# A hybrid encoder block in split fp32: seven units of its matrix products take a fifth pair of k tiles through Strassen's seven products, with four split buffers in place of five

## The chip, the cores and the metric

The kernel runs on one core of one Trainium2 chip. The time is in microseconds (us) of device time of one execution. A core has a matrix engine (PE), a vector engine (DVE), a scalar engine (ACT), a general engine (POOL) and a queue engine for transfers (SP); each takes its instructions in program order, and instructions wait for one another across engines.

## The reference

x has 256 tokens of 2048 channels. All is fp32.

```python
z = rms_norm(x) @ w_in                 # hq hf hi hg | aq ak av | gates
y_a = hgrn2(q, k, v, log_g)            # 8 heads, chunks of 64
y_b = chunk_band_attention(aq, ak, av) # 16 heads of 64
gate_a, gate_b = split(sigmoid(gates))
h = x + (gate_a * (y_a @ w_branch_a) + gate_b * (y_b @ w_branch_b)) @ w_out
u = rms_norm(h)
h = h + square(relu(u @ w_up)) @ w_down    # 2048 -> 8192 -> 2048
return rms_norm(h)
```

## The kernel before

**Split fp32.** PE multiplies in a rounded type (fp32r). An fp32 number is kept as two of these, a high part (the number, rounded by a cast) and a low part (what the cast left), and `mm3` (L138) makes one product of three matmuls, high by high, high by low (of the weights), low by high: L139, L140, L141. One such matmul is a 128x128 left tile by 128x512 weights into a PSUM bank. Activations are split once; weights are streamed from HBM and split as they come: a raw piece of 128x1024 (two k tiles of 512 columns, 512 KB) is loaded by SP (`piece`, L208), and `split` (L90) casts it to `wh` on ACT (L91) and subtracts to `wl` on DVE (L92). `parts` (L220) does this for a piece; `buf` (L201) gives the buffers, four each of `wh` and `wl`, and from unit gb0 on a fifth, in the pool "fifth", for every fifth split. A split whose buffer is still read by PE waits on ACT, and the DVE behind it.

**A unit** (class `Unit`, L774) is a product of 256 rows by 2048 k by two groups of 512 columns (n = 0 and 1), into four banks (m, n). The first eight of its 16 k tiles go by the Strassen-Winograd scheme: the eight blocks' products become seven, named by the banks they go to and the weights they take: 11A, 22A, 12C, 11D, 21A, 21B, 21D. A is the piece pair of k tiles 0 to 3 and n = 0, B of n = 1, D of k tiles 4 to 7 and n = 0, C of n = 1; each is summed in place between products, on DVE (`sums`, L843: A - B, then A - C; the signs are in the left sides) or by accumulating DMAs that POOL issues (`sent`, L848). A product is two splits of two k tiles, 12 matmuls (`product`, L807). The left sides of 22A, 12C, 21A and 21B are the sums S5, S4, S2, S7, made by `combos` (L735) and split like the rest. The other eight k tiles, 8 to 15, are plain: an item (n, (k, k+1)) is one split and 12 matmuls (`plain`, L853; `ITEMS`, L772).

**The order** is written by hand in `run` (L887): 11A, a late item of the unit before, sums A - B, 22A, the last late item and the end of the unit before (`rest`), then the "seconds" 12C and 11D (in turned order where no late item is left and the unit is not `spread`), sums A - C, a plain item, 21A, a plain item, 21B, two plain items, 21D, two plain items. The two items (1, (12, 13)) and (1, (14, 15)) go late, into the next unit. The letters of the next unit are loaded after 21A, 21B and 21D. Steps (`u.step`) put other work between: the turning and splitting of h (`h_blocks`, L1131: matmuls `tp_h` on PE, `hw` and `act_h` on DVE), or of the activations u. A scheduler keeps the order per engine nearly as written; splits and sums are issued early (`high_priority`), so that they stand ahead in their queues, and wait there for buffers.

**The units** are av, qk, ga0, ga2, gb0, gb2 (input projection, its gates), wo0, wo2 (output projection), and for each quarter qd of the 8192 hidden channels up{qd}0, up{qd}2, dn{qd}0, dn{qd}2. Where a unit's down projection ends, ACT copies the bank to `y` (L1211), and POOL adds it to h by a DMA. In gb0 and gb2 the gates of the unit before are evicted on ACT (`gate_gb`, L729). In names of tiles, `wl_up10p11D` is the low part of a piece of D in unit up10, product 11; `wl_up10r_8` that of the plain item with k tiles 8 and 9.

Of the kernel before, what the change touches and what calls it, by code (L numbers as in the profile page):

```python
# [50 lines left out]
def tile_hybrid_block(  # L51
# [714 lines left out]

    def evict(dst, acc):
        with tc.high_priority(offset=2000):
            nc.vector.tensor_tensor(dst, acc, dst, op=ALU.add)
# [3 lines left out]

    class Unit:  # L774


        def __init__(self, lhs, S, w, n0, what, done, kt0=0, apart=NC, steps=lambda: (), start=5, fresh=None, held=False, tail=False):
# [4 lines left out]
            self.raw, self.dma, self.c, self.items, self.steps = {}, {}, {}, list(ITEMS), []  # L782
# [104 lines left out]
    def run(u, then=None):  # L887
# [18 lines left out]
        if not late and not u.spread:  # L906
            seconds.reverse()
# [23 lines left out]
        u.plain(1, (8, 9))  # L931
# [10 lines left out]
        u.plain(1, (10, 11))  # L942
# [15 lines left out]
        u.plain(0, (10, 11))  # L958
# [103 lines left out]
    for gates, c, col, what, fresh in ((ga, 0, C_GA, "ga", None), (ga, 2, C_GA, "ga", None), (gb, 0, C_GB, "gb", ("21",)), (gb, 2, C_GB, "gb", ())):  # L1062
# [114 lines left out]
    for qd in range(NQ):  # L1177
# [3 lines left out]
        def turns(c0, uT=uT, rs=rs, Su=Su, blocks=blocks, qd=qd):  # L1181

            def one(c, m):
# [11 lines left out]

        for c in range(0, 4, 2):
            def done(m, n, acc, c=c, rs=rs, qd=qd):
                t = token(f"r{qd}{c}{n}{m}")
                with tc.high_priority(offset=2000):
# [117 lines left out]
```

## Time and profile before

| | |
|---|---|
| median of 3 runs | 1369.27 us (1367.44 to 1372.15) |
| the profiled execution | 1368.19 us, its span 1366.5 us |
| granted clock of PE | 0.999 |
| PE busy | 1356.7 us, 99% of the span |
| DVE busy | 1122.1 us, 82% |
| ACT busy | 948.6 us, 69% |
| POOL busy | 150.5 us, 11% |
| moved by DMA | 333.75 MB, 244 GB/s |

The profile is one execution: each row of a timeline gives the start from the span's beginning, the duration, engine, line, operation, out<-in, and in brackets the idle time before it with what ended it. Matmuls overlap, so what one costs is read from start to start. The groups' rows give busy time and the mean of one in ns. 1.7 us of the execution lie around the span.

### The profile page before, as it was taken

Reading aid. Unit: us, or ns where it says so; the run is one execution under the profiler, and the core shown is the slowest. Engines: PE = TensorE matmul, PEld = TensorE weight load, DVE = VectorE, ACT = ScalarE, POOL = GpSimd, SP = SyncE. Lnnn points to the kernel's source line nnn. Section 1 sums busy time; section 2 is a strip of 40 time slices with the busy share of each in tenths; the row PEclk is TensorE's granted clock in tenths of the full one; section 3 lists DMA queues with packets and bytes.
Section 4 is the critical chain, followed back from the end, with each engine's and each line's share of the span. In section 5 each row is a group of like instructions: output and inputs, shape, how many; then the busy total and the mean of one; then the engine's idle time right before and its main releaser. Section 6 shows DMA issues by size and latency. Waiting matters only on the chain.

```text
span 1366.5 us, 19044 instructions
## 1 busy us (share of the span) xinstructions
PE 1356.7 (99%) x6791; PEld 1123.1 (82%) x6791; DVE 1122.1 (82%) x1302; ACT 948.6 (69%) x1247; POOL 150.5 (11%) x231
## 2 busy tenths in 40 slices
PE   9999999999999999999999999999999999999997
PEld 7888888878778888888888888888888888888886
DVE  7888977887787775798998987789787888878886
ACT  6877765776777664455778766687666876668864
POOL 4000000111111000010121112100111002110210
PEclk9999999999999999999999999999999999999999
DMA  9754557788886986669899889988899888998892
GB/s 324 246 186 157 178 179 265 217 219 246 261 222 169 295 293 208 184 155 317 290 263 284 222 260 298 297 242 228 263 279 301 253 246 240 282 299 258 259 280 105
DMA packets 128895, 333.75 MB, mean 244 GB/s; under 512 B 11152, under 2 KB 12176, under 8 KB 128416
## 3 DMA queue, kind: packets, MB, share of 16 engines
q1 hardware_dynamic: 107936, 265.59, 56.4%
q0 software_dynamic: 20144, 66.14, 24.7%
q8 instruction: 53, 0.87, 0.3%
q10 hardware_dynamic: 720, 0.81, 0.2%
q14 instruction: 42, 0.34, 0.1%
HBM read 271.67 MB, written 10.49 MB: 206 GB/s over the span
## 4 chain that ended last, share of the span: by engine, by line
PE 98%; DMA 1%; ACT 0%; DVE 0%; issue 0%; SPq 0%; POOLq 0%; POOL 0%; ACTq 0%; DVEq 0%
PE acc_hf L181 2%; PE acc_hq L181 2%; PE tp_u L109 1%; PE acc_hg L139 1%; PE acc_qkc L139 1%; PE acc_hg L141 1%; PE acc_ba L141 1%; PE acc_hi L140 1%; PE acc_hi L139 1%; PE acc_bb L139 1%; PE acc_hi L141 1%; PE acc_hg L140 1%; PE acc_bb L141 1%; PE acc_ba L140 1%; PE acc_bb L140 1%; PE acc_ba L139 1%
## 5 line engine op out<-in xcount | busy, mean ns | idle before, releaser
L181 PE MATMUL acc_hf<-act_x,wh_hf 128*128 128x512 f32 x128 | 40.6, 399 | 0.4 <-DVE f L195 0.4
L181 PE MATMUL acc_hq<-act_x,wh_hq 128*128 128x512 f32 x128 | 40.5, 398 | 0.0
L91 ACT CAST wh_bb<-raw_bb 128x1024 fp32r<-128x1024 f32 x16 | 16.9, 1054 | 23.3 <-PE acc_ba L141 17.5
L92 DVE TENSOR_TENSOR wl_bb<-raw_bb,wh_bb 128x1024 fp32r<-128x1024 f32 x16 | 19.6, 1224 | 14.8 <-ACT wh_bb L91 14.7
L91 ACT CAST wh_ba<-raw_ba 128x1024 fp32r<-128x1024 f32 x16 | 16.8, 1053 | 19.9 <-PE acc_bb L141 13.8
L92 DVE TENSOR_TENSOR wl_ba<-raw_ba,wh_ba 128x1024 fp32r<-128x1024 f32 x16 | 19.6, 1223 | 10.8 <-ACT wh_ba L91 10.8
L186 PEld LDWEIGHTS acc_hq<-act_x,wl_hq 128*128 128x128 f32 x128 | 23.4, 188 | 6.1 <-DVE wl_hq L92 0.9
L186 PEld LDWEIGHTS acc_hf<-act_x,wl_hf 128*128 128x128 f32 x128 | 23.4, 188 | 6.0 <-DVE wl_hf L92 0.9
L1212 POOL DMA_DIRECT2D hd<-y x24 | 26.2, 1156 | 1.8 <-ACT y L1211 1.3
L92 DVE TENSOR_TENSOR wl_hf<-raw_hf,wh_hf 128x1024 fp32r<-128x1024 f32 (+2 forms) x21 | 20.3, 968 | 6.7 <-ACT wh_hf L91 6.7
L92 DVE TENSOR_TENSOR act_u<-tp_u,act_u 128x512 fp32r<-128x512 f32 x32 | 21.9, 685 | 4.7 <-ACT act_u L91 4.2
L139 PE MATMUL acc_bb<-wh_bb,act_yb 128*128 128x512 f32 x64 | 25.2, 393 | 0.0
L186 PE MATMUL acc_hq<-act_x,wl_hq 128*128 128x256 f32 x128 | 24.7, 280 | 0.4 <-DVE wl_hq L92 0.4
L186 PE MATMUL acc_hf<-act_x,wl_hf 128*128 128x256 f32 x128 | 24.7, 279 | 0.4 <-DVE wl_hf L92 0.4
L139 PE MATMUL acc_hg<-wh_hg,act_x 128*128 128x512 f32 x64 | 25.1, 392 | 0.0
L139 PE MATMUL acc_hi<-wh_hi,act_x 128*128 128x512 f32 x64 | 25.0, 391 | 0.0
L141 PE MATMUL acc_hg<-wh_hg,act_x 128*128 128x512 f32 x64 | 24.9, 390 | 0.0
L141 PE MATMUL acc_ba<-wh_ba,act_ya 128*128 128x512 f32 x64 | 24.9, 389 | 0.0
L141 PE MATMUL acc_hi<-wh_hi,act_x 128*128 128x512 f32 x64 | 24.9, 389 | 0.0
L140 PE MATMUL acc_hi<-wl_hi,act_x 128*128 128x512 f32 x64 | 24.9, 389 | 0.0
L140 PE MATMUL acc_hg<-wl_hg,act_x 128*128 128x512 f32 x64 | 24.9, 389 | 0.0
L139 PE MATMUL acc_ba<-wh_ba,act_ya 128*128 128x512 f32 x64 | 24.9, 389 | 0.0
(1996 smaller groups left out, 5226.6 us busy)
## 6 DMA issues: line engine op xcount, KB each, us to landing
raw_hi<-in_w_in_n_dram SPq DMA_DIRECT2D x16, 512.0 KB, 4.2
raw_hg<-in_w_in_n_dram SPq DMA_DIRECT2D x16, 512.0 KB, 4.3
raw_ba<-in_w_branch_a_dram SPq DMA_DIRECT2D x16, 512.0 KB, 4.6
raw_bb<-in_w_branch_b_dram SPq DMA_DIRECT2D x16, 512.0 KB, 4.7
raw_hf<-in_w_in_t_dram SPq DMA_DIRECT2D x12, 512.0 KB, 4.5
raw_hq<-in_w_in_t_dram SPq DMA_DIRECT2D x12, 512.0 KB, 5.5
hd<-y POOLq DMA_DIRECT2D x24, 256.0 KB, 7.4
raw_aq<-in_w_in_t_dram SPq DMA_DIRECT2D x8, 512.0 KB, 3.8
```

The costliest lines, as they stand in the source:

```text
L91: casts[:] = [(copy or nc.scalar.copy)(hi, src)]
L92: return nc.vector.tensor_tensor(lo, src, hi.bitcast(F32), op=ALU.subtract)
L109: nc.tensor.transpose(tp[:, j, :], src[:, j * P:(j + 1) * P], ident)
L139: nc.tensor.matmul(acc, hi, wh, start=first, stop=False, skip_group_check=True)
L140: nc.tensor.matmul(acc, hi, wl, start=False, stop=False, skip_group_check=True)
L141: newest[:] = [nc.tensor.matmul(acc, lo, wh, start=False, stop=last, skip_group_check=True)]
L181: newest[:] = [nc.tensor.matmul(acc[cb], wh[:, cb * P:(cb + 1) * P], r.rearrange("p u t -> p (u t)"), start=kt == 0, stop=last)]
L186: newest[:] = [nc.tensor.matmul(acc[cb][:, 0:T], wl[:, cb * P:(cb + 1) * P], r[:, 0, :], start=False, stop=False)]
L1212: nc.gpsimd.dma_start(hd[n][m], t, accum_op=ALU.add)
```

## The change

In seven units, gb2, up10, up20, up30, dn02, dn12 and dn22 (`five=True`), k tiles 8 and 9 join the Strassen part as a fifth pair, one k tile on each side. Each of the seven products then takes a fifth k tile: 7 mm3 in place of the 8 of the items (0, (8, 9)) and (1, (8, 9)). The raw pieces are the same two, of k tiles 8 and 9 for n = 0 (X) and n = 1 (Y), now loaded by `load5` into one buffer each of the pool "fifth"; a new `half` splits one k tile of them (128x512) into a buffer of full size, half of which stays empty. The sums of the fifth tiles are four adds of 128x512 a unit on DVE, issued after a product's first split (L854). `fifths` makes the fifth tiles of S5, S7, S2 and S4, once each for x, h and the u of three quarters. S7 is now kept in a part of the split left side that no product reads, and the split of that block is left out where it is made from the turns; the fourth step of x's sums comes after the product ak.

The fifth split buffer goes, for all units from gb0 on. A five unit leaves one late item in place of two, and the seconds are turned (11D ahead of 12C) where fewer than two are left; so up10, up20, up30 and up12, up22, up32 have no plain item between 22A, 11D and 12C. In five units A - C waits for the last low of the first second. PE has 5976 instructions in place of 5997 in program order, DVE 1366 for 1278, ACT 1205 for 1169; POOL and SP have as many as before. Lines move: L846 is now L890, L804 L841, L834 L878, L1211 L1266, L1142 L1194, L769 L796.

```diff
     def buf(tag, what):
-        if "fifth" in homes:
-            taken[tag] += 1
-        last = taken[tag] > 0 and taken[tag] % 5 == 0
-        return (homes["fifth"] if last else wpool).tile([P, 2 * NC], F32R, name=f"{tag}_{what}", tag=tag, bufs=1 if last else 4)
+        return wpool.tile([P, 2 * NC], F32R, name=f"{tag}_{what}", tag=tag, bufs=4)
...
+    def half(raw, a, what):
+        made = [buf(t, what)[:, 0:NC] for t in ("wh", "wl")]
+        with tc.high_priority(offset=2000):
+            lows.append(split(*[t.rearrange("p (c n) -> p c n", n=T) for t in made], view5(raw, a)))
+        return made
...
         def final(i, s):
-            t = home.tile([P, 4, 2, P], F32R, name=f"S{i}_{what}", tag=f"S{i}", bufs=1)
+            if i == 7:
+                t = lhs[0][:, :, :, P:2 * P]
+            else:
+                t = home.tile([P, 4, 2, P], F32R, name=f"S{i}_{what}", tag=f"S{i}", bufs=1)
...
+    def fifths(lhs, what, home, made):
+        a = token(f"a9_{what}").rearrange("p (j t) -> p j t", t=T)
+        x = lhs[2][:, 0:2].bitcast(F32)
+        nc.vector.tensor_tensor(a, x[:, :, 0, :], x[:, :, 1, :], op=ALU.add)
+        c = fours(token(f"c9_{what}"))
+        (a00, a10), (a01, a11) = [[a[:, j, m * P:(m + 1) * P] for m in range(NM)] for j in range(2)]
+        nc.vector.tensor_tensor(c[:, 0], a10, a11, op=ALU.subtract)
...
+        t = home.tile([P, 4, 2, P], F32R, name=f"S9_{what}", tag="S9", bufs=1)
+        split(t[:, :, 0, :], t[:, :, 1, :], c)
...
+    ITEMS5 = [(1, (10, 11)), (1, (12, 13)), (0, (10, 11)), (0, (12, 13)), (0, (14, 15)), (1, (14, 15))]
+    FIFTH = {"A": ("X", 0), "D": ("X", 1), "B": ("Y", 0), "C": ("Y", 1)}
+    SUMS5 = {("22", "A"): "B", ("21", "A"): "C", ("21", "B"): "C", ("21", "D"): "A"}
...
         def product(self, i, name, left, first=False):
...
                     wh, wl = parts(raw, f"{self.what}p{i}{name}{g}")
+                if not g and self.five and (i, name) in SUMS5:
+                    dst, src = [view5(self.raw[r], a) for r, a in (FIFTH[name], FIFTH[SUMS5[i, name]])]
+                    with tc.issue_after(lows[-1].ins), tc.high_priority(offset=2000):
+                        nc.vector.tensor_tensor(dst, dst, src, op=ALU.add)
                 for a in range(2):
                     mm3(self.c[i], *left(g + a), wh[:, a], wl[:, a], first and not g + a, False)
+            if self.five:
+                raw, a = FIFTH[name]
+                mm3(self.c[i], *left(4), *half(self.raw[raw], a, f"{self.what}p{i}{name}5"), False, False)
...
-        if not late and not u.spread:
+        if len(late) < 2 and not u.spread:
             seconds.reverse()
...
         seconds[0]()
+        behind_first = lows[-1]
         u.step(next(at))
         seconds[1]()
         with ExitStack() as es:
-            if u.spread:
-                es.enter_context(tc.issue_after(lows[-1].ins))
+            if u.spread or u.five:
+                es.enter_context(tc.issue_after((lows[-1] if u.spread else behind_first).ins))
             u.sums("A", "C")
         u.sent("D", "A")
         u.step(next(at))
-        u.plain(1, (8, 9))
+        u.plain(1, (10, 11) if u.five else (8, 9))
...
-            u.plain(0, (10, 11))
+        if not u.five:
+            u.plain(0, (10, 11))
...
         if then:
             then.load("D")
+            then.load5("X")
...
-        late.append(lambda: u.plain(1, LATE[0]))
+        if not u.five:
+            late.append(lambda: u.plain(1, LATE[0]))
         late.append(rest)
```

Three places of DVE's order are shown, before and after. First, unit up10 around its seconds: `raw_up10A` rows are the sums A - C, `_r_8` and `_r_10` the first plain item.

```order
878 L846 TENSOR_TENSOR raw_up10A_7833<-raw_up10A_7833,raw_up10C_7882 128x1024
879 L92 TENSOR_TENSOR wl_up10p12C_8080<-raw_up10C_7880,wh_up10p12C_8079 128x1024
880 L92 TENSOR_TENSOR wl_up10p12C_8090<-raw_up10C_7882,wh_up10p12C_8089 128x1024
881 L92 TENSOR_TENSOR wl_up10p11D_8100<-rawd_up10D_7939,wh_up10p11D_8099 128x1024
882 L92 TENSOR_TENSOR wl_up10p11D_8110<-rawd_up10D_7941,wh_up10p11D_8109 128x1024
883 L92 TENSOR_TENSOR wl_up10r_8_8124<-rawp_up10r_8_7975,wh_up10r_8_8123 128x1024
```

The same place after the change, with X and Y the fifth pieces:

```order
914 L92 TENSOR_TENSOR wl_up10p11D_8163<-rawd_up10D_8021,wh_up10p11D_8162 128x1024
915 L92 TENSOR_TENSOR wl_up10p11D_8173<-rawd_up10D_8023,wh_up10p11D_8172 128x1024
916 L92 TENSOR_TENSOR wl_up10p11D_8183<-rawx_up10X,wh_up10p11D_8182 128x512
917 L890 TENSOR_TENSOR raw_up10A_7915<-raw_up10A_7915,raw_up10C_7970 128x1024
918 L92 TENSOR_TENSOR wl_up10p12C_8190<-raw_up10C_7970,wh_up10p12C_8189 128x1024
919 L92 TENSOR_TENSOR wl_up10p12C_8200<-raw_up10C_7972,wh_up10p12C_8199 128x1024
920 L92 TENSOR_TENSOR wl_up10p12C_8210<-rawy_up10Y,wh_up10p12C_8209 128x512
921 L890 TENSOR_TENSOR raw_up10A_7917<-raw_up10A_7917,raw_up10C_7972 128x1024
922 L92 TENSOR_TENSOR wl_up10r_10_8221<-rawp_up10r_10_8059,wh_up10r_10_8220 128x1024
```

11D has come ahead of 12C, both sums A - C have moved between them and the plain item, and two halves have been added.

Second, unit gb2 at the same place, before and then after:

```order
558 L92 TENSOR_TENSOR wl_gb2p11D_4864<-rawd_gb2D_4707,wh_gb2p11D_4863 128x1024
559 L92 TENSOR_TENSOR wl_gb2p11D_4874<-rawd_gb2D_4709,wh_gb2p11D_4873 128x1024
560 L846 TENSOR_TENSOR raw_gb2A_4599<-raw_gb2A_4599,raw_gb2C_4648 128x1024
561 L846 TENSOR_TENSOR raw_gb2A_4601<-raw_gb2A_4601,raw_gb2C_4650 128x1024
562 L92 TENSOR_TENSOR wl_gb2r_8_4888<-rawp_gb2r_8_4743,wh_gb2r_8_4887 128x1024
```

After:

```order
568 L92 TENSOR_TENSOR wl_gb2p11D_4899<-rawd_gb2D_4718,wh_gb2p11D_4898 128x1024
569 L92 TENSOR_TENSOR wl_gb2p11D_4909<-rawd_gb2D_4720,wh_gb2p11D_4908 128x1024
570 L92 TENSOR_TENSOR wl_gb2p11D_4919<-rawx_gb2X,wh_gb2p11D_4918 128x512
571 L890 TENSOR_TENSOR raw_gb2A_4598<-raw_gb2A_4598,raw_gb2C_4657 128x1024
572 L890 TENSOR_TENSOR raw_gb2A_4600<-raw_gb2A_4600,raw_gb2C_4659 128x1024
573 L92 TENSOR_TENSOR wl_gb2r_10_4930<-rawp_gb2r_10_4756,wh_gb2r_10_4929 128x1024
```

The half of 11D is added ahead of the two sums.

Third, unit up00, where DVE evicts h (`h_3_0`, `h_3_1`) and the turned tiles (`hw`, `act_h`), from the first split of 11D on, before and then after:

```order
741 L92 TENSOR_TENSOR wl_up00p11D_6662<-rawd_up00D_6473,wh_up00p11D_6661 128x1024
742 L769 TENSOR_TENSOR h_3_1_6614<-acc_wo2c_6177,h_3_1_6614 128x512
743 L1142 TENSOR_TENSOR hw_0_6626<-tp_h_6621,vt 128x512
744 L92 TENSOR_TENSOR wl_up00p11D_6672<-rawd_up00D_6475,wh_up00p11D_6671 128x1024
745 L846 TENSOR_TENSOR raw_up00A_6333<-raw_up00A_6333,raw_up00C_6403 128x1024
746 L92 TENSOR_TENSOR act_h_6620<-hw_0_6626,act_h_6620 128x4x128
747 L1142 TENSOR_TENSOR hw_1_6656<-tp_h_6651,vt 128x512
748 L92 TENSOR_TENSOR wl_up00r_8_6697<-rawp_up00r_8_6512,wh_up00r_8_6696 128x1024
749 L92 TENSOR_TENSOR wl_up00p21A_6725<-raw_up00A_6331,wh_up00p21A_6724 128x1024
750 L92 TENSOR_TENSOR act_h_6620<-hw_1_6656,act_h_6620 128x4x128
751 L1142 TENSOR_TENSOR hw_0_6691<-tp_h_6686,vt 128x512
752 L92 TENSOR_TENSOR wl_up00p21A_6735<-raw_up00A_6333,wh_up00p21A_6734 128x1024
```

After, from the second split of 11D on (ahead of it stand `h_3_0`, `h_3_1`, `hw_0`, the first split of 11D and `act_h`):

```order
759 L92 TENSOR_TENSOR wl_up00p11D_6698<-rawd_up00D_6502,wh_up00p11D_6697 128x1024
760 L1194 TENSOR_TENSOR hw_1_6682<-tp_h_6677,vt 128x512
761 L890 TENSOR_TENSOR raw_up00A_6360<-raw_up00A_6360,raw_up00C_6430 128x1024
762 L92 TENSOR_TENSOR act_h_6646<-hw_1_6682,act_h_6646 128x4x128
763 L92 TENSOR_TENSOR wl_up00r_8_6723<-rawp_up00r_8_6538,wh_up00r_8_6722 128x1024
764 L1194 TENSOR_TENSOR hw_0_6717<-tp_h_6712,vt 128x512
765 L1194 TENSOR_TENSOR hw_1_6745<-tp_h_6740,vt 128x512
766 L92 TENSOR_TENSOR wl_up00p21A_6751<-raw_up00A_6358,wh_up00p21A_6750 128x1024
767 L92 TENSOR_TENSOR act_h_6711<-hw_0_6717,act_h_6711 128x4x128
768 L92 TENSOR_TENSOR act_h_6711<-hw_1_6745,act_h_6711 128x4x128
769 L92 TENSOR_TENSOR wl_up00p21A_6761<-raw_up00A_6360,wh_up00p21A_6760 128x1024
```

The first split of 11D has moved behind the evictions of h, and two more evictions of turned tiles stand ahead of 21A.

More of the change, by code (lines that the diff above doesn't have):

```diff
@@ L781, in __init__ @@
             self.spread, self.fresh = fresh is not None, fresh or ()
[L782 removed]
+            self.raw, self.dma, self.c, self.items, self.steps = {}, {}, {}, list(ITEMS5 if five else ITEMS), []
+            self.five = five
         def load(self, name):
@@ L941, in run @@
         u.step(next(at))
-        u.plain(1, (10, 11))
+        u.plain(1, (12, 13) if u.five else (10, 11))
         u.less("12", u1)
@@ L951, in run @@
             then.load("C")
+            then.load5("Y")
         u.step(next(at))
-        u.plain(0, (8, 9))
+        u.plain(0, (10, 11) if u.five else (8, 9))
         u.less("22", u2)
@@ L987, in rest @@
             u.end(1)
-        late.append(lambda: u.plain(1, LATE[0]))
+        if not u.five:
+            late.append(lambda: u.plain(1, LATE[0]))
         late.append(rest)
     Sx = {}
-    for f in combos(xT, "x", tk, Sx):
+    x_sums = combos(xT, "x", tk, Sx)
+    for f in x_sums[:3]:
         f()
@@ L1046, in tile_hybrid_block @@
         scaled("k0", rstd, m, acc_k[m])
+    x_sums[3]()
     yb += [new_act(f"yb{g}") for g in range(2)]
@@ L1067, in done @@
             gates[c + n][m] = sigmoid(token(f"gate_{what}{c + n}{m}", tkb if what == "gb" else None), acc, m)
-        units.append(Unit(lambda: xT, lambda: Sx, w_in_t, col + c * NC, f"{what}{c}", done, steps=gate_steps.pop(0) if gate_steps else lambda: (), fresh=fresh, held=what == "gb" and not c))
+        units.append(Unit(lambda: xT, lambda: Sx, w_in_t, col + c * NC, f"{what}{c}", done, steps=gate_steps.pop(0) if gate_steps else (lambda: ()) if c else lambda: [(KD, lambda: fifths(xT, "x", tk, Sx))],
+                          fresh=fresh, held=what == "gb" and not c, five=what == "gb" and c > 0))
     for i in range(2):
@@ L1190, in one @@
                     nc.scalar.copy(blocks[m, c], tp)
-                split(hi[:, :, m * P:(m + 1) * P], lo[:, :, m * P:(m + 1) * P], tp)
+                if c or not m:
+                    split(hi[:, :, m * P:(m + 1) * P], lo[:, :, m * P:(m + 1) * P], tp)
             return [(c, lambda c=c, m=m: one(c, m)) for c in (c0, c0 + 1) for m in range(NM)] + [
-                (c0 + 1, f, 7) for f in ([] if c0 else combos(uT, f"u{qd}", tk, Su, blocks))]
+                (c0 + 1, f, 7) for f in ([] if c0 else combos(uT, f"u{qd}", tk, Su, blocks))] + [
+                (99, lambda: fifths(uT, f"u{qd}", tk, Su), 7)] * (c0 > 0 and qd < NQ - 1)
         for c in range(0, 4, 2):
@@ L1204, in tile_hybrid_block @@
             units.append(Unit(lambda: hT, lambda: Sh, w_up, qd * (FF // NQ) + c * NC, f"up{qd}{c}", done,
-                              steps=(lambda turns=turns: turns(0)) if c else (lambda: ()) if qd else (lambda: h_blocks(2)), start=3 if c else 0, held=not qd and not c))
+                              steps=(lambda turns=turns: turns(0)) if c else (lambda: ()) if qd else (lambda: h_blocks(2)), start=3 if c else 0, held=not qd and not c, five=qd > 0 and not c))
         def out_of(m, n, acc, c=slice(0, NC), last=last, qd=qd):
@@ L1267, in tile_hybrid_block @@
                               lambda m, n, acc, *c, n0=n0, out_of=out_of: out_of(m, n0 + n, acc, *c), kt0=qd * KD,
-                              steps=(lambda: ()) if n0 else (lambda turns=turns, last=last: turns(2) + [(3, finals)] * last),
-                              start=0, tail=last and n0 == 2))
+                              steps=(lambda qd=qd: [(99, lambda: fifths(hT, "h", sp, Sh))] * (not qd)) if n0 else (lambda turns=turns, last=last: turns(2) + [(3, finals)] * last),
+                              start=3 if n0 else 0, tail=last and n0 == 2, five=n0 == 2 and not last))
     for u, then in zip(units, units[1:] + [None]):
```

24 lines of the change are left out of this document (19 added, 5 removed).

## The prediction

> **What bounds the kernel now.** I read the page first. The columns are busy time, share of the span and instructions.
>
> ```profile
> PE 1356.7 (99%) x6791; PEld 1123.1 (82%) x6791; DVE 1122.1 (82%) x1302; ACT 948.6 (69%) x1247; POOL 150.5 (11%) x231
> PE 98%; DMA 1%; ACT 0%; DVE 0%; issue 0%; SPq 0%; POOLq 0%; POOL 0%; ACTq 0%; DVEq 0%
> ```
>
> PE is busy throughout, and the chain that ended last is 98% PE: the span is the sum of its matmuls. The view of waits says whether anything feeds it late; its columns are total us, times, longest.
>
> ```profile
> PE ps_warm L81 <- DVE warm L79: 1.1, 1, 1.1
> PE acc_hf L186 <- DVE wl_hf L92: 0.4, 1, 0.4
> PE acc_hq L186 <- DVE wl_hq L92: 0.4, 1, 0.4
> PE acc_hf L181 <- DVE f L195: 0.4, 1, 0.4
> ```
>
> These 2.3 us are all, none in a product that the change touches. So no stall can go away: a gain can only come from fewer matmuls, and a loss from new waits. The timeline gives the price of a matmul, where units dn02 and up10 begin, and the windows view the unit up10 whole (PE, PEld, DVE, ACT, POOL busy, PE clock, DMA share, GB/s).
>
> ```profile
> 811.11 0.39 PE L139 MATMUL acc_dn02c<-wh_dn02p11A,act_u 128*128 128x512 f32 x1
> 811.33 0.39 PE L140 MATMUL acc_dn02c<-wl_dn02p11A,act_u 128*128 128x512 f32 x1
> ...
> 851.90 0.39 PE L139 MATMUL acc_up10c<-wh_up10p11A,act_h 128*128 128x512 f32 x1
> 851.90:892.70 40.80, 40.80 (x181) 33.79 (x180) 32.36 (x29) 27.60 (x31) 6.93 (x9) 1.00 1.00 284
> ```
>
> From 811.11 to 851.90 lie 180 matmuls in 40.79 us: 0.2267 us from start to start, though one lasts 0.39 (they overlap). In such a unit DVE is busy 32.4 of 40.8 us and ACT 27.6; DMA is at 1.00.
>
> **What is removed.** k tiles 8 and 9 take 7 products of one k tile where they took 8: three matmuls fewer in each of seven units, 21 in all. 21 x 0.2267 = **-4.76 us**, 0.35% of the time, the most that the change can give.
>
> [...]
>
> **What is added.** More and smaller splits on ACT and DVE. Their prices, on DVE:
>
> ```profile
> 682.16 0.68 DVE L769 TENSOR_TENSOR h<-acc_wo2c,h 128x512 f32<-128x512 f32 x1
> 682.76 1.21 DVE L846 TENSOR_TENSOR raw_up00A<-raw_up00A,raw_up00B 128x1024 f32<-128x1024 f32 x1
> 683.89 0.68 DVE L769 TENSOR_TENSOR h<-acc_wo2c,h 128x512 f32<-128x512 f32 x1
> L92 DVE TENSOR_TENSOR act_u<-tp_u,act_u 128x512 fp32r<-128x512 f32 x32 | 21.9, 685 | 4.7 <-ACT act_u L91 4.2
> ```
>
> From start to start, in a queue, a 128x512 takes 0.60 us and a 128x1024 1.13 to 1.14; alone 0.685 and 1.22. A five unit replaces two splits of 128x1024 by seven of 128x512 and adds four sums of 128x512: 7 x 0.60 - 2 x 1.14 + 4 x 0.60 = 4.3 us. No row shows the sums' 128x2x256 form; its bounds are 0.60 and 1.14, and I take 0.60, the row of as many elements; none lies in the stretches walked below. Either way 32.4 + 4.3 to 6.5 stays under the 40.1 us that PE then needs, so on the mean DVE keeps up. S9 of the left side (five times, about 2 us, -0.6 for each skipped split) sits in stretches with idle DVE; its cover is the lead of the splits there. I cost both at nothing. The same holds for x_sums[3], moved behind the ak product. No DMA is added.
>
> **What is lost is lead.** With a buffer fewer, a split waits until PE is done with the fourth before it; and a half-filled buffer covers 0.68 us of PE, not 1.36. How long release to ready takes is seen in up10, on PE, ACT and DVE:
>
> ```profile
> 862.56 0.39 PE L141 MATMUL acc_dn02c<-wh_dn02r,act_u 128*128 128x512 f32 x1
> 862.78 0.39 PE L139 MATMUL acc_up10c<-wh_up10p12C,S_h 128*128 128x512 f32 x1
> 862.98 0.59 ACT L1211 COPY y<-acc_dn02c 128x512 f32<-128x512 f32 x1 [0.64 <-PE acc_dn02c L141]
> 863.47 1.05 ACT L91 CAST wh_up10r<-rawp_up10r 128x1024 fp32r<-128x1024 f32 x1
> 864.55 1.23 DVE L92 TENSOR_TENSOR wl_up10r<-rawp_up10r,wh_up10r 128x1024 fp32r<-128x1024 f32 x1 [1.44 <-ACT wh_up10r L91]
> ```
>
> ACT starts 0.20 after PE's last matmul; copy to next cast 0.49; cast 1.05, then 0.03 to DVE, then 1.23. I walked the new order with these, and four places come out late.
>
> *up10, up20, up30.* T = 0 where 22A begins on PE. These units now run 22A, 11D, 12C with no plain item between, three products of 15 matmuls: 45 x 0.2267 = 10.20 us, and the low of the plain split r10 is wanted by the second matmul after, at 10.43. ACT first has the last y copy of the unit before (0.20 to 0.69), then casts 11D (to 1.74), so DVE begins 11D's low at 1.80. From there to r10 its queue has six of 128x1024 (11D twice, a sum A - C, 12C twice, a sum) and the two halves of 128x512: 6 x 1.14 + 2 x 0.60 = 8.04; r10 ends at 1.80 + 8.04 + 1.22 = 11.06. Stall 0.63 each, **1.9 us** for three. After it 21A has over 1 us to spare.
>
> *gb2.* Both sums A - C stand between 11D and the plain item, as before (ACT's row first, then DVE's, then PE's):
>
> ```profile
> 478.91 0.69 ACT L729 ACTIVATE gate_gb<-acc_gb0c,rstd 128x512 f32<-128x512 f32 x1 [0.54 <-PE acc_gb0c L141]
> ...
> 477.82 1.23 DVE L92 TENSOR_TENSOR wl_gb2p11D<-rawd_gb2D,wh_gb2p11D 128x1024 fp32r<-128x1024 f32 x1 [0.67 <-ACT wh_gb2p11D L91]
> 478.96 2.36 DVE L846 TENSOR_TENSOR raw_gb2A<-raw_gb2A,raw_gb2C 128x1024 f32<-128x1024 f32 x2
> 481.23 1.22 DVE L92 TENSOR_TENSOR wl_gb2r<-rawp_gb2r,wh_gb2r 128x1024 fp32r<-128x1024 f32 x1
> ...
> 484.38 0.39 PE L140 MATMUL acc_gb2c<-wl_gb2r,act_x 128*128 128x512 f32 x1
> ```
>
> Before, r was ready at 482.45 for 484.38. Now 11D's first split takes the buffer that PE frees only when 12C begins (T = 0), behind a gate: gate 0.20 to 0.79, cast to 1.84, DVE from 1.88: 11D 2 x 1.14, half 0.60, sums 2 x 1.13, r10 1.22 end at 8.24. PE wants it after 31 matmuls, at 7.03. **1.2 us.**
>
> *gb0*, which is not a five unit but has four buffers:
>
> ```profile
> 438.06 0.57 ACT L804 COPY acc_gb0c<-acc_gb0c 128x512 f32<-128x512 f32 x1 [0.30 <-PE acc_gb0c L141]
> 438.55 1.05 ACT L91 CAST wh_gb0r<-rawp_gb0r 128x1024 fp32r<-128x1024 f32 x1
> ...
> 441.20 1.22 DVE L92 TENSOR_TENSOR wl_gb0r<-rawp_gb0r,wh_gb0r 128x1024 fp32r<-128x1024 f32 x1
> ...
> 443.58 0.39 PE L140 MATMUL acc_gb0c<-wl_gb0r,act_x 128*128 128x512 f32 x1
> ```
>
> Its second 11D split now needs a buffer of 22A and stands behind that copy: cast at 438.55, low at 439.64, the sums at 440.78 and 441.91, r from 443.05 to 444.27, against 443.58. **0.7 us.**
>
> *up00*, where DVE evicts h and the turned tiles among the splits:
>
> ```profile
> 693.74 0.60 PE L109 MATMUL tp_h<-ident,h 128*128 128x128 f32 x4
> 694.32 0.68 DVE L769 TENSOR_TENSOR h<-acc_wo2c,h 128x512 f32<-128x512 f32 x1
> ...
> 703.34 0.60 PE L109 MATMUL tp_h<-ident,h 128*128 128x128 f32 x4
> 703.69 0.47 PE L139 MATMUL acc_up00c<-wh_up00p21A,S_h 128*128 128x512 f32 x1
> ```
>
> T = 0 at 693.74. The first 11D split moves behind the evictions. From 0.20 DVE has nine 128x512 (5.4), five 128x1024 (5.7), then 21A's second low: ready at 12.5. PE has 45 matmuls and four groups of transposes at 0.35 ahead of it: 11.6. **0.9 to 1.0 us.**
>
> For dn02, dn12 and dn22 the same walk leaves 0.5 us to spare, since a plain item lies between; for wo0, wo2, up12 to up32 and dn10 to dn30 0.9 or more. I cost them at nothing; without that cover each would lose what is missing, once.
>
> **Sum.** -4.76 + 1.9 + 1.2 + 0.7 + 1.0 = +0.04 us. The profiled execution took 1368.19 us (span 1366.5, 1.7 around it) and would come out at 1368.2; it lies 1.1 under the median of 1369.27, which I move by the same sum: **1369.3 us**. About 0.3%, 4.1 us, is what a measurement of this kernel tells from no change.
>
> [...]
>
> **Rivals.** *The cover holds* (15%): ACT and DVE run further ahead than I walked, as the absence of any wait before might suggest, and stalls stay under 0.65 in all. Then 1369.27 - 4.76 + 0 to 0.65: 1364.5 to 1365.2. Against it: the queue of up10 needs 9.26 us of DVE for 8.63 of cover, by rows alone.
>
> *Piece X comes late* (slower, 17%). X has one buffer. For up10, up20 and up30 it is loaded when 21D's half of the unit before is split. Counted from that unit's 21B on PE, this is by my walk at 7.2; 21B, a plain item, 21D, two plain items and two pairs of 11A (78 matmuls, 17.68 us) later PE wants the new half, whose split must start by 16.4: 9.2 us to land. The landing times of up10's D pieces and of the y accumulates (min, median, max):
>
> ```profile
> DMA to landing us min/median/max: 6.1/6.6/9.8
> DMA to landing us min/median/max: 5.9/7.4/11.3
> ```
>
> At the medians it is hidden; at 11.3, with DMA share 1.00, each of three units waits 2.1 us: 1369.3 + 6.3 = 1375.6. It decides from 9.2 us on.
>
> *The clock falls* (3%): every window shows 1.00 now. [...]
>
> That the matmuls don't go is no rival: the order has 21 rows fewer on PE.
>
> **How the numbers follow.** My forecast has 65%: 1369.3, by itself 1366 to 1373 (stalls from a third to twice the walk's). The range's ends are the cover's 1364.5 and X's 1375.6; only the clock, and what I left out, lies beyond. Faster by over 0.3% asks for stalls under 0.65: 0.15. Slower by over 0.3% asks for X, the clock, or walks that missed 4 us: 0.20. Between: 0.65.
>
> **What would show it.** The waits of PE on DVE's lows: acc_up10c, acc_up20c, acc_up30c on wl r10 at about 0.6, acc_gb2c at 1.2, acc_gb0c at 0.7, acc_up00c at 1.0, and PE busy 4 to 5 us shorter. Wrong would be: no PE waits and a span near 1362; waits on ACT casts of X behind a DMA; a clock under 1.00; or waits in dn02 and the units that I cost at nothing.

## The result and the profile after

The changed kernel takes 1377.95 us (median of 6 runs, 1376.47 to 1380.89), the one before 1368.92 (6 runs); the ratio is 1.0068, 95% interval 1.0057 to 1.0078. It is slower by 9 us where no change was forecast, and lies above the range's end of 1375.6.

First the page of the changed kernel, busy time and the chain that ended last:

```profile
PE 1359.1 (99%) x6770; PEld 1119.8 (81%) x6770; DVE 1154.5 (84%) x1390; ACT 963.1 (70%) x1282; POOL 150.9 (11%) x231
PE 63%; DVE 2%; issue 2%; DMA 2%; ACT 1%; POOL 0%; POOLq 0%; ACTq 0%; DVEq 0%
```

The 21 matmuls are gone from PE's count (6791 to 6770), and yet PE is busy 2.4 us longer: a matmul lasts 0.39 us and the next starts after 0.23, so starts that are up to 0.16 us late count as busy, and so do slow matmuls. The chain is no longer PE alone. The view of PE's waits, which before had 2.3 us in all, says where (lines of the span's first microseconds and the shortest wait are left out):

```profile
PE acc_dn30c L139 <- ACT u_dn L841: 2.0, 1, 2.0
...
PE acc_dn02c L140 <- DVE wl_dn02r L92: 0.8, 1, 0.8
PE acc_dn12c L140 <- DVE wl_dn12r L92: 0.8, 1, 0.8
PE acc_dn22c L140 <- DVE wl_dn22r L92: 0.8, 1, 0.8
PE acc_gb2c L140 <- DVE wl_gb2r L92: 0.6, 1, 0.6
PE acc_dn02c L139 <- ACT wh_dn02r L91: 0.5, 1, 0.5
PE acc_dn12c L139 <- ACT wh_dn12r L91: 0.4, 1, 0.4
PE acc_gb0c L139 <- ACT acc_gb0c L841: 0.4, 1, 0.4
...
PE acc_up00c L140 <- DVE wl_up00p21A L92: 0.3, 1, 0.3
```

gb2 and up00 wait on the lows that were forecast, each for less; gb0 waits too, but on a copy of ACT and not on a low. No wait at r10 of the up units; instead the late item of the unit before (`wl_dn02r` and its like) comes late, in the same three units, and dn30 has a wait that I did not have at all. The waits of ACT for transfers, from 810 us to 1320 us, show what stands behind both (columns: total, times, longest); first the kernel before:

```profile
ACT wh_up20r L91 <- DMA rawp_up20r<-in_w_up_dram: 3.8, 2, 2.7
ACT wh_dn12r L91 <- DMA rawp_dn12r<-in_w_down_dram: 3.3, 1, 3.3
ACT wh_up10r L91 <- DMA rawp_up10r<-in_w_up_dram: 3.1, 2, 2.7
ACT wh_up30r L91 <- DMA rawp_up30r<-in_w_up_dram: 2.9, 2, 2.1
ACT wh_dn02r L91 <- DMA rawp_dn02r<-in_w_down_dram: 1.8, 1, 1.8
ACT wh_dn30r L91 <- DMA rawp_dn30r<-in_w_down_dram: 1.5, 1, 1.5
```

And the changed kernel:

```profile
ACT wh_up10p11A L91 <- DMA rawx_up10X<-in_w_up_dram: 5.6, 1, 5.6
ACT wh_up20p11A L91 <- DMA rawx_up20X<-in_w_up_dram: 5.3, 1, 5.3
ACT wh_up30p11A L91 <- DMA rawx_up30X<-in_w_up_dram: 4.7, 1, 4.7
ACT wf L1314 <- DMA wf<-in_norm_final_w_dram: 2.5, 1, 2.5
```

ACT waited for transfers before, too, 2 to 3 us at a time, and PE did not notice: the splits ahead covered it. Now it waits 5 us for X and 2.5 for wf, the weights of the final norm, and PE notices.

How X becomes a wait of PE stands in the timeline of up10: X's landing, then ACT, DVE and PE.

```profile
DMA to landing us min/median/max: 9.7/9.7/9.7
858.21 0.62 ACT L91 CAST wh_up10p11A<-rawx_up10X 128x512 fp32r<-128x512 f32 x1 [5.58 <-DMA rawx_up10X<-in_w_up_dram]
858.74 1.07 ACT L1266 COPY y<-acc_dn02c 128x512 f32<-128x512 f32 x2
859.69 1.06 ACT L91 CAST wh_dn02r<-rawp_dn02r 128x1024 fp32r<-128x1024 f32 x1
860.78 1.23 DVE L92 TENSOR_TENSOR wl_dn02r<-rawp_dn02r,wh_dn02r 128x1024 fp32r<-128x1024 f32 x1
859.61 0.50 PE L140 MATMUL acc_up10c<-wl_up10p11A,act_h 128*128 128x512 f32 x1
859.95 0.40 PE L141 MATMUL acc_up10c<-wh_up10p11A,act_h 128*128 128x512 f32 x1
860.80 0.50 PE L139 MATMUL acc_dn02c<-wh_dn02r,act_u 128*128 128x512 f32 x1 [0.46 <-ACT wh_dn02r L91]
862.07 0.50 PE L140 MATMUL acc_dn02c<-wl_dn02r,act_u 128*128 128x512 f32 x1 [0.76 <-DVE wl_dn02r L92]
```

X itself is hardly late for PE: the half of 11A runs 0.12 us behind its turn. But ACT takes its queue in order, and behind X stand two copies of y and the cast of the late item. From X's cast (858.21) to the end of the item's low (862.01) it is 3.8 us. PE had matmuls for 1.96 us of them, the rest of 11A and one high part, and wanted the low at 860.17: 1.9 us are lost.

In dn30, ACT and PE again:

```profile
1300.24 1.91 ACT L1314 ACTIVATE wf<-wf 128x2048 f32<-128x2048 f32 x1 [2.52 <-DMA wf<-in_norm_final_w_dram]
1302.06 0.57 ACT L841 COPY u_dn<-acc_dn30c 128x512 f32<-128x512 f32 x1
...
1302.68 0.50 PE L139 MATMUL acc_dn30c<-wh_dn30p21B,act_u 128*128 128x512 f32 x1 [1.97 <-ACT u_dn L841]
```

The copy of a bank, which PE needs, stands behind the scaling of wf, and that behind wf's load. In the order of ACT the scaling and the copy have moved ahead of the cast of `r_8`. Before:

```
wh_dn30p21B   act_u   wh_dn30r_8   wf<-wf   COPY u_dn   wh_dn30r_10
```

After, and in the kernel with nothing but a buffer fewer (below):

```
wh_dn30p21B   wf<-wf   COPY u_dn   wh_dn30r_8   wh_dn30r_10
```

And the load goes out later. POOL has it behind the accumulating DMAs of D, which wait for 11D's low; before, then after:

```profile
1281.23 0.85 POOL L851 DMA_DIRECT2D rawd_dn30D<-raw_dn30A  x1 [0.89 <-DMA raw_dn32A<-in_w_down_dram]
1281.76 0.88 POOL L1258 DMA_DIRECT2D wf<-in_norm_final_w_dram  x1
```

```profile
1288.43 0.85 POOL L895 DMA_DIRECT2D rawd_dn30D<-raw_dn30A  x1 [1.97 <-DVE wl_dn30p11D L92]
1288.97 0.88 POOL L1313 DMA_DIRECT2D wf<-in_norm_final_w_dram  x1
```

dn30's first matmul starts at 1269.8 before and 1274.2 after: wf goes out 12.0 us into the unit, then 14.8. It lands after 10.2 us before and 11.3 after, so 22.2 and 26.1 us into the unit. Before, the copy ended 0.55 us ahead of the matmul that needs it (1295.63 for 1296.18); now it ends 2.1 us after PE is through with the matmuls ahead of that one. The new order alone doesn't hold the copy up: in both orders it comes right behind the scaling.

What each stretch lost is worked out from the starts of the units' first matmuls: its length less that of before, plus 0.68 us for each five unit in it; dn32 is taken to its last matmul. "up10" is dn02, up10 and up12 together, since late items move between them; up20 and up30 are likewise four units each. The last column is the ratio to the kernel before, with its interval. The kernels are those of the next section.

| us lost in | gb0 | gb2 | wo | up00 | up10 | up20 | up30 | dn30, dn32 | ratio |
|---|---|---|---|---|---|---|---|---|---|
| forecast | 0.7 | 1.2 | 0 | 1.0 | 0.6 | 0.6 | 0.6 | 0 | |
| changed kernel | 0.7 | 1.6 | 0.2 | 0.6 | 2.4 | 2.1 | 1.4 | 3.9 | 1.0068 (1.0057 to 1.0078) |
| e1, half of 11A behind the late item | 0.7 | 1.5 | 0.2 | 1.1 | 0.8 | 0.7 | 0.7 | 4.3 | 1.0044 (1.0027 to 1.0061) |
| e2, wf scaled late | 0.7 | 1.6 | 0.2 | 0.6 | 1.8 | 1.3 | 1.8 | 1.6 | 1.0061 (1.0041 to 1.0081) |
| e4, both | 0.7 | 1.6 | 0.2 | 1.0 | 0.7 | 0.7 | 0.7 | 2.7 | 1.0021 (1.0012 to 1.0031) |
| e3, only a buffer fewer | 0.7 | 1.0 | 0.2 | 1.6 | 1.7 | 2.2 | 2.0 | 1.6 | 1.0089 (1.0074 to 1.0104) |
| e5, five buffers from wo0 | 0.7 | 1.5 | 2.2 | 0.4 | 1.7 | 2.9 | 1.7 | 0.0 | 1.0050 (1.0035 to 1.0065) |
| e6, the same and e1 | 0.8 | 1.6 | 2.6 | 0.9 | 0.6 | 1.7 | 1.2 | 0.9 | 1.0025 (1.0015 to 1.0036) |
| e7, up units without | 0.7 | 1.6 | 0.5 | 1.4 | 4.5 | 4.2 | 0.9 | 4.4 | 1.0091 (1.0062 to 1.0119) |
| e8, X freed early | 0.8 | 1.2 | 0.9 | 1.4 | 0.4 | 0.4 | 0.4 | 4.1 | 1.0024 (1.0015 to 1.0034) |
| f1, e8 and wf loaded early | 0.8 | 1.7 | 0.6 | 1.4 | 0.4 | 0.6 | 0.6 | 0.6 | 1.0003 (0.9994 to 1.0011) |
| f2, f1 and the room lent | 0.0 | 0.0 | 0.0 | -0.1 | 0.3 | 0.7 | 0.4 | 0.0 | 0.9979 (0.9970 to 0.9988) |

For the changed kernel the row sums to 12.9; less 4.76 it is 8.2, and the two spans (1374.8 and 1366.5) differ by 8.3. Ahead of gb0 the profiles differ by up to 1 us from one execution to the next, which the table leaves out. Each row is one execution, up to 3.4 us faster (e2) or 1.5 us slower (e8) than its kernel's median, and a stretch moves by itself: e2 changes nothing in the three up stretches, and they differ from the changed kernel's by 0.4 to 0.7 us. Differences of that size between two rows show nothing by themselves.

### The profile page after: what moved, and what is told of

It reads as the page before. It is cut to its first block, busy times and chain, and to the rows that moved or that the text cites. A ratio compares the mean times of both kernels' runs of the same rounds, so it can differ in the third digit from the quotient of the medians.

```text
span 1374.8 us, 19153 instructions
## 1 busy us (share of the span) xinstructions
PE 1359.1 (99%) x6770; PEld 1119.8 (81%) x6770; DVE 1154.5 (84%) x1390; ACT 963.1 (70%) x1282; POOL 150.9 (11%) x231
## 4 chain that ended last, share of the span: by engine, by line
PE 63%; DVE 2%; issue 2%; DMA 2%; ACT 1%; POOL 0%; POOLq 0%; ACTq 0%; DVEq 0%
PE acc_ba L141 1%; PE acc_bb L139 1%; PE acc_bb L141 1%; PE acc_bb L140 1%; PE acc_ba L139 1%; PE acc_ba L140 1%; PE acc_wo2c L141 1%; PE acc_wo2c L139 1%; PE acc_dn00c L139 1%; PE acc_dn32c L140 1%; PE acc_dn10c L139 1%; PE acc_dn20c L141 1%; PE acc_dn32c L139 1%; PE acc_dn12c L140 1%; PE acc_up02c L141 1%
## 5 line engine op out<-in xcount | busy, mean ns | idle before, releaser
L1267 POOL DMA_DIRECT2D hd<-y x24 | 22.5, 976 | 50.8 <-ACT y L1266 46.7
L140 PE MATMUL acc_ba<-wl_ba,act_ya 128*128 128x512 f32 x64 | 24.9, 389 | 0.0
L140 PE MATMUL acc_bb<-wl_bb,act_yb 128*128 128x512 f32 x64 | 24.9, 389 | 0.0
```

What stands on the lines that cost most here:

```text
L140: nc.tensor.matmul(acc, hi, wl, start=False, stop=False, skip_group_check=True)
L1267: nc.gpsimd.dma_start(hd[n][m], t, accum_op=ALU.add)
```

## The experiments

My theory after the result: two transfers, X and wf, come late and hold ACT. The rival: with four buffers the splits are late anyway, and the waits for X and wf only stand where others would.

**e1: the half of 11A behind the late item**, in up10, up20 and up30.

```diff
-        u.product("11", "A", u.block(0, 0), True)
+        u.product("11", "A", u.block(0, 0), True, len(late) != 1)
+        if len(late) == 1:
+            q()
+            u.fifth("11", "A", u.block(0, 0))
         u.begun("21", "11")
```

> In up10, up20 and up30 the half of 11A that needs piece X comes behind the late plain item of the unit before, on ACT, DVE and PE; nothing else moves. Theory 'two transfers' (X, and the weight row wf, arrive late in front of ACT, which takes its instructions in order): the stalls at the start of the three units, 5.9 us in the trace of the changed kernel, go; 1378.0 - 5.9 = 1372.1 us, no wait of ACT for X. Rival 'buffers' (with four buffers the splits are late anyway, and the wait for X only stands where another would): my walk's stall of 0.63 us at the plain item r10 comes back in each unit, so 4.0 us go, 1374.0, and PE waits in acc_up10c on the low of r10.

1374.20 us (4 runs), 3.8 us less: the rival's number. ACT's wait for X falls from 5.6 to 0.4 us in up10, and 0.7 us are left in each of the three stretches, 0.5 of it at 12C's low and 0.1 at r10. So 3.7 of the 5.9 us are X's. The rest is near the size of the stall that my walk had found, but not at its place.

**e2: wf scaled late.** In this kernel and in e4 a part of the last multiplication runs before wf has its factor, so that factor is missing in some columns.

```diff
-            nc.scalar.activation(fin["w"], fin["w"], AF.Copy, scale=D ** 0.5)
...
-[(3, finals)] * last
+[(3, finals), (99, scale_w, 99)] * last
```

> ACT's scaling of the final norm weights (wf) moves from the middle of dn30 into dn32; its load stays where it is. Theory 'two transfers': PE's wait of 2.0 us in dn30 goes, and with it the 1.7 us in which the matmuls after it run at 0.43 us each; 1378.0 - 3.9 = 1374.1. Rival: the clock there falls for another reason, or the D pieces are late anyway, and only the wait goes: 1376.0.

1376.56 us, but its 4 runs spread from 1373.18 to 1379.98, so this time alone decides nothing. The profile does: the wait in dn30 and the slow matmuls behind it are gone (3.9 to 0.0 in dn30), and 1.6 us appear in dn32, where a plain item of dn30 comes late. The wait had held up work that was itself nearly late. This profile is of the fastest of the four; whether the slower ones lost their time there is not shown.

**e4: both.**

> Both moves together. Theory 'two transfers': 1378.0 - 9.8 = 1368.2, as fast as before; what is left of the loss is 0.7 us in gb0, 1.6 in gb2 and 0.7 in up00, against 4.76 gained, so 1366 to 1369. Rival 'buffers': 1370 or more, with waits at r10 in three units.

1371.30 us (10 runs), 3 us above what my theory gave and in the rival's range, though the waits that it put at r10 are, as in e1, mostly at 12C. The two moves add up in the up units and not in dn30 and dn32, which keep 2.7 us: there ACT waits for dn30's own plain pieces, and its longest wait is 5.05 us for one of them. The theory of two transfers is too narrow.

**e3: the kernel before with four buffers, and nothing else.**

```diff
-        if "fifth" in homes:
-            taken[tag] += 1
-        last = taken[tag] > 0 and taken[tag] % 5 == 0
-        return (homes["fifth"] if last else wpool).tile(..., bufs=1 if last else 4)
+        return wpool.tile(..., bufs=4)
```

> The kernel before with four split buffers instead of five from gb0 on, nothing else (no fifth pair). In its order ACT scales wf ahead of the cast of the plain item r8 in dn30, as in the changed kernel and unlike before. Theory 'two transfers': gb0 0.7, up00 0.7 and the wf wait with its slow matmuls 3.9: 1368.9 + 5.3 = 1374.2. Rival 'the fifth pair delays wf' (its extra work on ACT and DVE, not the order, makes the wait): only gb0 and up00, 1370.3.

1380.44 us (4 runs): 12 us slower than before, more than twice what I expected, and slower than the changed kernel. On top of four buffers, then, the fifth pair is if anything a gain, of 0.2% or so (the intervals just meet). What is lost in the up units here has no X in it:

```profile
877.64 1.05 ACT L91 CAST wh_up10r<-rawp_up10r 128x1024 fp32r<-128x1024 f32 x1
882.30 1.05 ACT L91 CAST wh_up10r<-rawp_up10r 128x1024 fp32r<-128x1024 f32 x1 [3.61 <-DMA rawp_up10r<-in_w_up_dram]
883.25 1.04 ACT L91 CAST wh_up10p21D<-rawd_up10D 128x1024 fp32r<-128x1024 f32 x1
884.20 0.58 ACT L800 COPY u_up<-acc_up10c 128x512 f32<-128x512 f32 x1
```

It is the same thing: a piece lands late, ACT stands still, and the copy that PE waits for (`u_up`, 0.9 us in PE's waits) is two places behind. The wait for this piece is 3.61 us; before, with a buffer more, the longest for up10's plain pieces was 2.7 and cost nothing. wf's wait is here too (1.8 us), in the order shown above, and its load goes out 14.8 us into dn30 as in the changed kernel: it comes with the buffer, not with the fifth pair. But PE waits 1.3 us for it here and no slow matmuls follow, so dn30 and dn32 lose 1.6 us and not 3.9; the wait is the buffer's, and its full price is not.

**e5 and e6: a fifth split buffer again**, from wo0 on, in the room of the fifth left tiles; e6 has e1's move as well.

```diff
+        if "sixth" in homes:
+            taken[tag] += 1
+        last = taken[tag] > 0 and taken[tag] % 5 == 0
...
-        t = home.tile([P, 4, 2, P], F32R, name=f"S9_{what}", tag="S9", bufs=1)
-        split(t[:, :, 0, :], t[:, :, 1, :], c)
+        t = token(f"S9_{what}").bitcast(F32R).rearrange("p (k t) -> p k t", t=P)
+        split(t, t, c)
```

> The changed kernel with a fifth split buffer again from wo0 on (gb0 and gb2 keep four). It gets the room by leaving out the store of the fifth left tiles of S5, S7, S2 and S4: their sums and their split are still made, but the products take another left tile of the same shape, so the output is not the reference's. Theory 'buffers': the lead comes back; up00 (0.7) and dn30 (3.9) lose their waits and X's late landing is covered by the split ahead of it, so 1378.0 - 4.6 - about 4 = 1369; the floor, with gb0 and gb2 left (2.3 us) and 4.76 gained, is 1366.4. Rival 'two transfers': X has its one buffer as before and still lands 9 to 10 us after its issue, ahead of the late item on ACT; its 5.9 us stay, 1373.4.

1375.09 us (4 runs). The wait in dn30 is gone (3.9 to 0.0), as both theories had it. In the up units nothing is won (5.9 us in the changed kernel, 6.3 here): ACT waits 5.3, 6.5 and 5.3 us for X. The buffer does not help against X, since X has one buffer of its own. There the theory 'buffers' fails and its rival holds. The 2.2 us in wo0 are this experiment's own; its new pool takes room that the gates have just left, which may be why, and no run shows it.

> The same fifth buffer from wo0 on (same part of the left sides left out), and 11A's half behind the late item in up10, up20 and up30. Both theories: no wait for X, none at 12C or r10, none in dn30; 1368.9 - 4.76 + 0.7 in gb0 + 1.6 in gb2 = 1366.4. If it stays above 1368.5, the fifth pair has a cost of its own that neither theory names.

1372.17 us (10 runs), above 1368.5. 2.6 us of it are those of the wo units again. The three up stretches lose 3.5 us even with five buffers, at 12C and r10, where my walk has the half splits. In up10 (0.6) ACT has no wait for X over 0.8 us; in up20 and up30 (1.7 and 1.2) it still waits 3.1 and 2.7 us for X, and what is the halves' there and what X's is not separated.

**e7: only gb2 and the down projections take the fifth pair.**

```diff
-five=qd > 0 and not c))
+five=False))
```

> Only gb2, dn02, dn12 and dn22 take the fifth pair; up10, up20 and up30 take plain items again; four buffers. X is then loaded two units ahead and can't be late. 2.04 us of the gain are given back. Theory 'two transfers': 1378.0 - 5.9 + 2.0 = 1374.1. Theory 'buffers': without X's wait the up units stall where they did with four buffers alone, 1.0 to 1.4 us each, so 1377.5 to 1378.5.

1382.48 us (4 runs, 1374.92 to 1383.73): slower than both said, though the fastest of the four comes near the number of 'two transfers'. The profile is of the slowest. In it, without X, up10 and up20 lose 4.5 and 4.2 us. ACT waits for a plain piece of up10:

```profile
ACT wh_up10r L91 <- DMA rawp_up10r<-in_w_up_dram: 5.4, 1, 5.4
```

That piece took 13.5 us from issue to landing, beside the accumulates of y (11.6) and D (15.6). So another piece can take X's part in this stage.

**e8: X freed early.** 21D takes its fifth tile first.

```diff
+            ahead = self.five and (i, name) == ("21", "D")
+            if ahead:
+                ...
+                self.fifth(i, name, left)
             for g, raw in zip((0, 2), self.raw[name]):
```

> The changed kernel, in which 21D of the five units takes its fifth tile first instead of last, so that X's buffer is free, and the next X loaded, some 2 us earlier; the order at the start of the next unit stays. Theory 'late X': X lands at 7 to 8 us into its wait instead of 9.7, ACT is held about 2 us less in three units, and what was 2.4, 2.1 and 1.5 us of stall falls to the 0.6 of the moved-half kernel or less: 1378.0 - 4 = 1374. Rival: the late item of the unit before is late for want of a buffer, whatever X does: 1377 to 1378.

1371.60 us (10 runs). X of up10 is issued 1.1 us earlier in the span (847.4 for 848.5) and 2.2 us earlier in unit dn02, which begins at 814.8 for 813.7; it lands after 9.5 us. ACT waits for it 3.5 us in place of 5.6, and the late item is in time:

```profile
856.98 0.62 ACT L91 CAST wh_up10p11A<-rawx_up10X 128x512 fp32r<-128x512 f32 x1 [3.49 <-DMA rawx_up10X<-in_w_up_dram]
857.51 1.07 ACT L1275 COPY y<-acc_dn02c 128x512 f32<-128x512 f32 x2
858.46 1.06 ACT L91 CAST wh_dn02r<-rawp_dn02r 128x1024 fp32r<-128x1024 f32 x1
```

What is left in the three stretches is 0.4 us each: 4.7 of 5.9 us went with one reordering that moves no work from one engine to another. The wo units and up00 lose 1.5 us more than in the changed kernel, which I have not followed up; and yet the median is 2.4 us under the theory's. A wait of ACT of 3.5 us is covered and one of 5.6 costs 2 us.

**f1: e8, with wf loaded early** and scaled behind the cast of 21A.

```diff
-            fin["w"] = apool.tile([P, D], F32, name="wf", tag="act")
-            nc.gpsimd.dma_start(fin["w"], ...)
-            nc.scalar.activation(fin["w"], fin["w"], AF.Copy, scale=D ** 0.5)
+            with tc.issue_after(casts[0].ins):
+                nc.scalar.activation(fin["w"], fin["w"], AF.Copy, scale=D ** 0.5)
...
+                [ahead(t) if last and not i else t for i, t in enumerate(turns(2))]
```

> The kernel in which X is freed early (1371.6 us), and wf is loaded some 30 us earlier, ahead of the accumulating DMAs of dn30 on POOL, and scaled on ACT behind dn30's cast of 21A. Theory 'late transfers hold ACT': PE's wait in dn30 (2.3 us) and the slow matmuls behind it (1.7 us) go, 1371.6 - 4 = 1367.6, within 0.3% of before. Rival 'dn30 is short of lead anyway' (the plain pieces of dn30 land late, as when wf was scaled late): only 1.3 to 2 us go, about 1370.

1369.19 us (11 runs), the kernel before in the same runs 1368.76: no difference. That lies between the theory's 1367.6 and the rival's 1370; by place the theory holds, as dn30 and dn32 go from 4.1 to 0.6. The load goes out 45 us earlier than in e8 (30 us ahead of dn30), and the scaling has moved too, so the two are not told apart.

**f2: f1, with the room of X and Y lent** as the fifth split buffer until dn00, and gb2 with plain items.

```diff
+        if homes.get("lent"):
+            taken[tag] += 1
+        last = homes.get("lent") and taken[tag] % 5 == 0
+        return (homes["fifth"] if last else wpool).tile(..., tag=f"raw{'xy'[tag == 'wl']}" if last else tag, bufs=1 if last else 4)
...
+        if then and then.five:
+            homes["lent"] = False
```

> As the one with wf ahead, but gb2 takes plain items again (six five units, 4.08 us gained), and the room of X and Y serves as the fifth split buffer from gb0 until dn00, where X and Y are first loaded. Theory: the waits in gb0, gb2, wo2 and up00 (0.7, 1.2, 0.7 and 1.5 us over before in the kernel with X freed early) go, 0.7 of the gain is given back: 1367.6 - 4.2 + 0.7 = 1364, faster than before by about 0.35%. Rival: lending the room costs waits of its own where it changes hands, and the fifth pair's waits in the up units grow as the rest gets faster: 1367 or more.

1366.03 us (11 runs) against 1368.76: ratio 0.9979 (0.9970 to 0.9988), faster than both kernels, 2 us above the theory's 1364 and 1 us under the rival's 1367. It keeps 2.7 of the 4.08 us that six five units can give; the table has 1.2 to 1.3 us of it in the up stretches. The five waits of PE that its view lists all lie at the start of the span; the longest two:

```profile
PE ps_warm L81 <- DVE warm L79: 1.1, 1, 1.1
PE acc_hf L181 <- DVE f L195: 0.8, 1, 0.8
...
```

## Why the prediction was wrong

**The gain was right.** 21 matmuls at 0.2267 us went: the changed kernel's losses sum to 12.9 us, and its span is 8.3 longer. I had 4.8 us of losses. Of the 8.1 us missing, about 4 are in the up units, about 4 in dn30, and little in the rest.

**gb0, gb2, up00: near in size, and in place for two of the three.** 0.7, 1.2 and 1.0 forecast; 0.7, 1.6 and 0.6 measured, with 0.2 in wo. In gb2 the walk was exact: with 12C beginning at 480.85, it has r10's low ending at 489.09, and the trace at 489.08. 0.9 us are lost there, and most of the rest at 21D's lows, which I had at nothing. In gb0 the walk's time is right and its wait did not occur:

```profile
438.75 0.50 PE L139 MATMUL acc_gb0c<-wh_gb0p12C,S_x 128*128 128x512 f32 x1 [0.38 <-ACT acc_gb0c L841]
443.10 1.22 DVE L92 TENSOR_TENSOR wl_gb0r<-rawp_gb0r,wh_gb0r 128x1024 fp32r<-128x1024 f32 x1
487.86 1.22 DVE L92 TENSOR_TENSOR wl_gb2r<-rawp_gb2r,wh_gb2r 128x1024 fp32r<-128x1024 f32 x1
```

The low ends at 444.32 (the walk: 444.27). But PE had already lost 0.7 us at 12C's first matmul, which waits for ACT's copy of a bank: before, it had four matmuls of 11D to run there, and now one, as 11D's low comes later. So the size in gb0 is luck. f2, which gives these stretches their buffer back, has none of these losses.

**The up units: the walk failed at its first row.** I walked from 22A on, with the late item ready at T = 0. It wasn't. The step that failed is the one that priced X: "At the medians it is hidden", with a threshold of 9.2 us and the overshoot as its price. X took 8.8 to 9.7 us, so it was at most 0.5 us over; the loss was 1.4 to 2.4 us a unit. The price of a late transfer on ACT is what stands behind it in the queue: copies, cast and low, 3.8 us in up10, less the 1.96 us of matmuls that PE had left. My rival had the place and, with a landing time of 11.3 us that did not occur, nearly the size (2.1 a unit), at a chance of 17%. The walk's own 0.63 us did not come at r10 (0.1 us there in the changed kernel); e1, with X moved, has 0.7 a unit, mostly at 12C. That the sizes agree does not show that the walk was right.

**dn30: missed.** "dn10 to dn30 0.9 or more. I cost them at nothing" held for dn10 and dn20 (0.0 us lost in both) and failed in dn30 for 3.9 us: I looked only at splits there, not at what else stands in ACT's and POOL's queues. That wf is scaled ahead of a cast instead of behind it could be read in the order before the run; that its load goes out 2.8 us later follows from the later low of 11D. e3 shows that the buffer alone does both, at a loss of 1.6 us; f1 that an earlier load, scaled earlier, cures it. The other 2.3 us in the changed kernel are a landing 0.7 us later and the slow matmuls behind the longer wait. That the clock falls I had at 3%: the kernel before shows no fall up to 1300 us (1.00 in every window of 100 us), and in the changed kernel the waits of up to 0.8 us in gb2 and the up units left it at 1.00; it fell once, in dn30, to 0.51 for 3.5 us.

**What lies under both.** I asked of each split only when its buffer comes free, and took every raw piece as landed. The trace of before had ACT waiting 2 to 3 us for pieces at a DMA share of 0.98 in dn02 and 1.00 in up10. The fifth buffer covered that. Its price, 12 us alone (e3), is larger than anything that I had for it. The loads there are late for two reasons, and the traces of up10, up20 and up30 have both. In e3 the fifth of the eight plain pieces goes out 27.1 to 27.3 us into its unit, before 20.8 to 21.9, and takes no longer to land (5.8 to 5.9 us; before 5.8 to 6.3): it is issued late. In e7 the fourth goes out earlier than before (12.3 to 12.6 us; before 13.9) and takes 13.5, 13.1 and 11.7 us to land in place of 9.0, 9.7 and 9.4. What holds SP up in e3, and which transfers slow the load in e7, is not shown.

## What to carry to other kernels

Before a buffer is taken away, read the waits of the engines that fill it, above all those for transfers, and not only of the one that is full: a wait that costs nothing is what the buffer is for. Price a late transfer by what is queued behind it on the engine that waits, down to the first thing that the full engine needs, and not by how late it lands. And walk an order from the work that is still open from the unit before, small instructions included.

## What the runs showed of the hardware

The clock rival came true in small, at one place. In the changed kernel's dn30, the windows view (PE, PEld, DVE, ACT, POOL busy, PE clock, DMA share, GB/s):

```profile
1300.50:1302.60 2.10, 0.21 (x1) 0.00 (x0) 0.00 (x0) 2.10 (x3) 0.54 (x1) 1.00 0.99 404
1302.60:1303.90 1.30, 1.22 (x5) 1.05 (x6) 0.99 (x2) 1.30 (x3) 0.00 (x0) 1.00 1.03 419
1303.90:1307.40 3.50, 3.50 (x10) 2.72 (x10) 3.20 (x3) 1.94 (x3) 0.00 (x0) 0.51 1.03 421
1307.40:1310.00 2.60, 2.60 (x13) 2.15 (x12) 1.93 (x2) 1.26 (x2) 0.00 (x0) 1.00 1.03 419
```

After 2.0 us without a matmul the first five run at full clock, then the granted clock is 0.51 for 3.5 us, and then 1.00 again. There the matmuls start 0.43 us apart instead of 0.23:

```profile
1304.32 0.63 PE L139 MATMUL acc_dn30c<-wh_dn30p21B,act_u 128*128 128x512 f32 x1
1304.75 0.63 PE L140 MATMUL acc_dn30c<-wl_dn30p21B,act_u 128*128 128x512 f32 x1
1305.17 0.63 PE L141 MATMUL acc_dn30c<-wh_dn30p21B,act_u 128*128 128x512 f32 x1
```

Some 1.7 us are lost in this way, nearly as much as in the wait: from 1302.68 to 1307.59 us 14 matmuls start, which at 0.2267 us take 3.2 us. In the profiles of all these kernels, every place at which two matmuls start 2.36 to 3.08 us apart (6 places in 4 kernels: one each in the changed kernel, e1 and e8, three in e7) is followed by six or seven matmuls that start 0.43 us apart, and none of those with 0.93 to 1.70 us (34 places) is; between 1.70 and 2.36 us these traces have no place. The shortest wait of PE among the six is 2.0 us, in the changed kernel, and the longest 2.7, in e7; the longest among the 34 are 1.3 us, in e3 and e5.
